# Block 0's gated products: multiplied, transposed and split ahead of the first fast pair, with the pair's first weights loaded early

## The chip, the core and the metric

The kernel runs on one core of one Trainium2 chip. The metric is the device time of one execution in microseconds, the median over several runs. The engines named here are PE (matrix products), DVE and POOL (elementwise work), ACT (casts and activations) and SP, which only issues transfers in this kernel. Each engine works through its own instructions in the order in which they are written, and waits for another engine or a transfer through semaphores.

## What is computed

One trunk layer on x of 256 tokens by 2048 channels, in float32 (the attention and convolution in between are left out):

```python
xn = rms_norm(h, norm1_g)
proj = xn @ w_in                       # q, k, v and the convolution's two gates
...
h = h + concat([att, u]) @ w_out
hn = rms_norm(h, norm2_g)
a  = hn @ w_gate                       # 2048 x 5632
bu = hn @ w_up                         # 2048 x 5632
h  = h + (silu(a) * bu) @ w_down       # 5632 x 2048
```

The change lies in the last four lines, at the seam between the first block of columns of the FFN and the others.

## The kernel before

**Products of split numbers.** Every float32 operand of a product is split into a high part (rounded to the multiplier's format fp32r) and a low part (the rest). A product is three matmuls: high by high, high by low, low by high. For weights, ACT casts the high part (`whi`, L334), and DVE subtracts to get the low part (`wlo`, L343). Part of the low halves are made by ACT and an accumulating transfer on POOL's queue instead (L337, L338). Activations have their halves in `lhi` and `llo`, or, for the normed state `hn`, in the forms that `make_forms` makes.

**Blocks.** The 5632 columns are 11 blocks of N = 512. Block 0 is plain: first all of `w_gate`, then all of `w_up`, 16 row tiles each, in chunks of two row tiles (one raw load of 0.5 MB, one cast, one subtract, 12 matmuls). Blocks 1 to 10 are fast blocks: part of their rows are multiplied in pairs by a scheme of seven products in place of eight. A pair needs one load of 1 MB (`load_pair`, tile `wb`), sums of its parts on DVE (`pair_sums`, `wt`, L1004 to L1006), a cast on ACT (`round_pair`, `wh`, L1010 and L1011) and a subtract on DVE (`split_pair`, `wl`, L1015 and L1016), and is then 21 matmuls (`multiply_pair`, L1032 to L1034). The remaining rows go in units of 12 matmuls (L1050, L1051, L1055). `FIRST = "gugusgsUsGsU"` gives the order of a half of block 1: g and u are units of the gate and of the up columns, s is a pair, and a capital letter is a unit whose low weights come by the transfer. So four units come ahead of block 1's first pair. The blocks form groups of 4, 4 and 3; behind each group stand its products with `w_down`.

**Order of work.** The tile framework keeps the order of the code for each engine. `run_chunks` sets that order: while it multiplies chunk t it runs loads, pair sums, casts and subtracts ahead by fixed numbers of chunks (`LOAD_AHEAD, DMA_AHEAD, SUMS_AHEAD, HI_AHEAD, LO_AHEAD = 9, 5, 5, 4, 3`), from `AHEAD` chunks before the first fast chunk on. Raw loads have four buffers. Everything else that must run beside the chunks is a generator which `resume()` moves on by a step, twice in every chunk or unit; `lag(n)` is n such steps.

**The seam.** Behind the residual's last columns, DVE, POOL and ACT make the second norm's factor (`rstd2`; L218 on POOL is its last step). Then `make_forms` works on `hn` step by step while PE multiplies the up half of block 0: it scales `hn`, and makes `chi`, `clo` for the units and `fhi`, `flo` for the pairs. `hn` lies in the two buffers of the pool `early` that `load_pair` uses for `wb` later. When the up half's sums are complete, `up_done` multiplies `a = ps * rstd2 * silu` on DVE (L872). `transposed` then transposes `a` on PE in two groups of four (L905, outputs `ps_a`), copies the high half on ACT and subtracts the low half on DVE (`llo`, L912). PE's accumulator banks for these transposes come from the same pool `acc_ps` as block 0's sums. The pair's products go into banks that these use as well, so it depends on `llo`.

For the fast blocks, `block_done` ends with the sum of the two halves and the gate (`sum`, L1152), waits some steps, and calls `transposed` as well: five steps, but three in the last block of each group (blocks 3, 7 and 10), with banks of the pool `aux_ps`.

Of the kernel before, what the change touches and what calls it, by code (L numbers as in the profile page):

```python
# [13 lines left out]
F32 = mybir.dt.float32  # L14
# [94 lines left out]
def tile_block(  # L109
# [345 lines left out]
    def run_chunks():  # L455
        n = len(chunks)
        pair_at.extend(i for i, c in enumerate(chunks) if "sides" in c)
        two_at.extend(i for i, c in enumerate(chunks) if "kind" in c and "sides" not in c)
        at = dict(part=0, dma=0, sums=0, round=0)
        first = next(i for i, c in enumerate(chunks) if "kind" in c)  # L460

        def until(what, do, stop, only=lambda c: True, may=lambda i: True):
            while at[what] < min(n, stop) and may(at[what]):
                if only(chunks[at[what]]):
                    do(at[what])
                at[what] += 1

        for t in range(n):
            if t >= first - AHEAD:
                until("part", part_of, t + 1 + LO_AHEAD)  # L470
                until("sums", sums_of, t + 1 + SUMS_AHEAD, may=may_sum)
                until("dma", round_of, t + 1 + DMA_AHEAD, lambda c: c["by_dma"])
                until("round", round_of, t + 1 + HI_AHEAD)
                load_until(t + 1 + LOAD_AHEAD)
            else:
                until("part", part_of, t + 1 + (1 if t < len(XPARTS) else AHEAD))
            part_of(t)
            chunks[t]["multiply"](chunks[t])
            if chunks[t].get("prompt") and chunks[t]["done"]:
                resume()  # L480
        while running:
            resume()
# [382 lines left out]

    def up_done(j, ps):
        fp = ffn["pool"]
        yield
        aa = []
        for m in range(NM):  # L870
            a = fp.tile([P, N], F32, tag=f"sum{2 + m}", name="a")
            dve.scalar_tensor_tensor(a, ps[m], rstd2[m], sil[m], ALU.mult, ALU.mult)  # L872
            aa.append(a)
        yield
        yield from transposed(j, aa)

    def group_of(j):
        return next((g for g in range(len(FGROUPS)) if j < sum(FGROUPS[: g + 1])), None)
# [15 lines left out]
    def transposed(j, aa):  # L894
        g = group_of(j)
        if g not in down:
            place(g)
        d = down[g]
        for t in range(N // P // 2):
            pool_, tag = (aux_ps, "aux") if j else (acc_ps, "acc")  # L900
            pt = pool_.tile([P, 2, S], F32, tag=tag, name="ps_a")
            for i in range(2):
                for m in range(NM):
                    c = (2 * t + i) * P
                    pe.transpose(pt[:, i, m * P : (m + 1) * P], aa[m][:, c : c + P], ident)  # L905
            if (j, t) in d["pairs"]:
                yield from pair_forms(j, t, pt)
            else:
                hi, lo = d["at"][j, t]
                act.copy(hi, pt)  # L910
                yield from lag(3 if j else 2)
                dve.tensor_tensor(lo, pt, hi.bitcast(F32), ALU.subtract)  # L912
            d["ready"].add((j, t))
            yield from lag(2 if j else 1)

    def pair_forms(j, t, pt):

        fp = ffn["pool"]
        q = down[group_of(j)]["pairs"].index((j, t))
        fhi, flo = (f[:, :, q] for f in down[group_of(j)]["forms"])  # L920
        a = fp.tile([P, 2, NM, P], F32, tag="sum0", name="af")
        act.copy(a, pt)
        a11, a21, a12, a22 = a[:, 0, 0], a[:, 0, 1], a[:, 1, 0], a[:, 1, 1]
        act.copy(fhi[:, :2], a[:, :, 0])
        act.activation(fhi[:, 2], a22, AF.Copy, scale=-1.0)
        yield from lag(2)
        f = fp.tile([P, 4, P], F32, tag="sum2" if j else "sum1", name="fs")
        dve.scalar_tensor_tensor(f[:, 1], a21, -1.0, a22, ALU.mult, ALU.subtract)
        dve.scalar_tensor_tensor(f[:, 2], f[:, 1], -1.0, a11, ALU.mult, ALU.subtract)
        dve.tensor_tensor(f[:, 3], a11, a21, ALU.subtract)  # L930
        dve.tensor_tensor(f[:, 0], a12, f[:, 2], ALU.subtract)
        act.copy(fhi[:, 3:], f)
        yield from lag(2)
        dve.tensor_tensor(flo[:, :2], a[:, :, 0], fhi[:, :2].bitcast(F32), ALU.subtract)
        dve.scalar_tensor_tensor(flo[:, 2], a22, -1.0, fhi[:, 2].bitcast(F32), ALU.mult, ALU.subtract)
        yield
        dve.tensor_tensor(flo[:, 3:], f, fhi[:, 3:].bitcast(F32), ALU.subtract)
# [2 lines left out]

    def make_forms():
        fp = ffn["pool"]
        rep = fp.tile([P, S], F32, tag="sum1", name="rep")
        for m in range(NM):
            act.activation(rep[:, m * P : (m + 1) * P], ident, AF.Identity, bias=rstd2[m], scale=0.0)
        yield
        ps = aux_ps.tile([P, N], F32, tag="aux", name="ps_r")
        for m in range(NM):
            pe.transpose(ps[:, m * P : (m + 1) * P], rep[:, m * P : (m + 1) * P], ident)
        yield  # L950
        rb = fp.tile([P, S], F32, tag="sum2", name="rb")
        act.copy(rb, ps[:, :S])
        yield
        for i in range(2):
            for k in range(0, HK, 4):
                t = hn[i][:, k : k + 4, :]
                dve.tensor_tensor(t, t, rb.unsqueeze(1).to_broadcast([P, 4, S]), ALU.mult)
                yield

        nr = HK - NS  # L960
        chi = fp.tile([P, 2 * nr, S], F32R, tag="chi", name="chi")
        clo = fp.tile([P, 2 * nr, S], F32R, tag="clo", name="clo")
        for i in range(2):
            act.copy(chi[:, i * nr : (i + 1) * nr], hn[i][:, NS:])
        yield
        for i in range(2):
            dve.tensor_tensor(clo[:, i * nr : (i + 1) * nr], hn[i][:, NS:],
                              chi[:, i * nr : (i + 1) * nr].bitcast(F32), ALU.subtract)
            yield
        forms.update(plain={k: (chi[:, i, :], clo[:, i, :]) for i, k in enumerate(REST)})  # L970
        a11, a21 = (hn[0][:, :NS, m * P : (m + 1) * P] for m in range(NM))
        a12, a22 = (hn[1][:, :NS, m * P : (m + 1) * P] for m in range(NM))
        fhi = fp.tile([P, 7, NS, P], F32R, tag="fhi", name="fhi")
        flo = fp.tile([P, 7, NS, P], F32R, tag="flo", name="flo")
        f = fp.tile([P, 7, NS, P], F32, tag="wh", name="sums", bufs=2)[:, :4]
        dve.scalar_tensor_tensor(f[:, 1], a21, -1.0, a22, ALU.mult, ALU.subtract)
        dve.scalar_tensor_tensor(f[:, 2], f[:, 1], -1.0, a11, ALU.mult, ALU.subtract)
        act.copy(fhi[:, 0], a11)
        act.copy(fhi[:, 1], a12)
        act.activation(fhi[:, 2], a22, AF.Copy, scale=-1.0)  # L980
        yield
        dve.tensor_tensor(f[:, 3], a11, a21, ALU.subtract)
        dve.tensor_tensor(f[:, 0], a12, f[:, 2], ALU.subtract)
        act.copy(fhi[:, 3:], f)
        yield
        for i, a in ((0, a11), (1, a12)):
            dve.tensor_tensor(flo[:, i], a, fhi[:, i].bitcast(F32), ALU.subtract)
        yield
        dve.scalar_tensor_tensor(flo[:, 2], a22, -1.0, fhi[:, 2].bitcast(F32), ALU.mult, ALU.subtract)
        yield  # L990
        dve.tensor_tensor(flo[:, 3:], f, fhi[:, 3:].bitcast(F32), ALU.subtract)
        forms.update(hi=fhi, lo=flo)

    def load_pair(c):
        c["b"] = early.tile([P, 4, N], F32, tag="wb", name="wb")
        src = weights([(w, k, col, N) for w, col in c["sides"] for k in c["ks"]])
        sp.dma_start(out=c["b"].rearrange("p k n -> p (k n)"), in_=src)

# [146 lines left out]
    def block_done(j, q):  # L1145
# [4 lines left out]
            dve.tensor_tensor(u[m], q[i], u[m], ALU.add)  # L1150
        for m in range(NM):
            dve.tensor_tensor(u[m], u[m], g[m], ALU.mult)  # L1152
        yield from lag(TO_TRANSPOSE if group_of(j) == group_of(j + 1) else 3)
        yield from transposed(j, u)

    def add_to_out(m, n, t):
# [58 lines left out]
    for g, nb in enumerate(FGROUPS):  # L1215
        for j in range(j0, j0 + nb):
            if j:
                gate_up_block(j, FIRST if j == 1 else ORDER)
                continue

            block("w_gate", j * N, range(KD), fh, silu_done)
            block("w_up", j * N, range(KD), fh, lambda ps, j=j: up_done(j, ps))
        for n in range(0, D // N, 2):
            down_block(g, n)
        j0 += nb
# [40 lines left out]
```

## Time and profile before

| | us |
|---|---|
| median of 3 runs | 1077.01 (1076.92 to 1077.07) |
| profiled execution | 1075.79 |
| its span | 1074.0 |
| PE busy | 1044.6 (97%) |
| DVE busy | 900.4 (84%) |
| ACT busy | 654.0 (61%) |
| POOL busy | 129.9 (12%) |
| mean granted clock of PE | 0.993 of full speed |

The span is the time from the first to the last instruction that the profiler recorded; the profiled execution's own time is 1.8 us more. The granted clock is the share of PE's full clock that the chip let it have; in the stretches of this trace that lie wholly in one state it is 1.00 or 0.50. In the rows of the timeline the brackets give the idle time of the engine ahead of the instruction, and what ended it. Names behind an arrow are the program's tiles.

### The profile page before, as it was taken

What the parts mean: (1) busy time and instruction counts of PE and PEld (TensorE: products, weight loads), DVE (VectorE), ACT (ScalarE), POOL (GpSimd) and SP (SyncE); (2) the same over time, 40 slices, a digit from 0 to 9 for tenths busy, and PEclk for the clock granted to TensorE, in tenths of its full rate; (3) what the DMA queues carried; (4) which work ended last, traced back from release to release, by engine and by line L of the source; (5) the groups of instructions that cost most, each with busy time, mean ns of one, the idle gap of its engine ahead of it and who ended that gap; (6) DMA issues with size and microseconds to landing.
All of it is one profiled execution on the core that took longest, in us unless ns stands there. A gap on an engine that the chain in (4) does not pass through costs nothing.

```text
span 1074.0 us, 13249 instructions
## 1 busy us (share of the span) xinstructions
PE 1044.6 (97%) x4780; PEld 861.5 (80%) x4780; DVE 900.4 (84%) x1124; ACT 654.0 (61%) x831; POOL 129.9 (12%) x176
## 2 busy tenths in 40 slices
PE   7999999999999996999999999999999999999898
PEld 7888888877888875787878888888878888888786
DVE  4799989898766677989887788899986897989994
ACT  6644566755756555575765465765755756658551
POOL 0020112200100100010101120100101121001011
PEclk9999999999999998999999999999999999999999
DMA  8656554454457566887959998979878999889774
GB/s 300 211 182 200 184 189 161 154 167 158 146 182 239 167 227 184 273 231 227 310 161 320 264 296 289 287 208 327 235 234 247 260 309 334 240 238 270 238 201 93
DMA packets 62445, 245.47 MB, mean 229 GB/s; under 512 B 6964, under 2 KB 8430, under 8 KB 54956
## 3 DMA queue, kind: packets, MB, share of 16 engines
q1 hardware_dynamic: 48576, 200.56, 52.8%
q0 software_dynamic: 13744, 44.05, 21.5%
q8 instruction: 37, 0.61, 0.2%
q14 instruction: 28, 0.23, 0.1%
q10 hardware_dynamic: 60, 0.03, 0.0%
HBM read 236.22 MB, written 8.39 MB: 228 GB/s over the span
## 4 chain that ended last, share of the span: by engine, by line
PE 55%; DVE 7%; issue 2%; ACT 1%; DMA 1%; DVEq 0%; SPq 0%; ACTq 0%
PE q L1050 10%; PE q L1051 10%; PE q L1055 10%; PE q L1032 8%; PE q L1033 8%; PE q L1034 8%; DVE wl L1016 1%; DVE wlo L343 1%; PE ps_a L905 1%; DVE wt L1004 1%; DMA wb<-in_wts_dram 1%; DVE wt L1005 0%; ACT whi L334 0%; DVE wl L1015 0%; ACT wh L1011 0%
## 5 line engine op out<-in xcount | busy, mean ns | idle before, releaser
L334 ACT CAST whi<-raw 128x1024 fp32r<-128x1024 f32 (+1 forms) x261 | 269.1, 1047 | 122.1 <-PE q L1051 59.2
L343 DVE TENSOR_TENSOR wlo<-raw,whi 128x1024 fp32r<-128x1024 f32 (+1 forms) x193 | 233.7, 1218 | 73.3 <-ACT whi L334 70.5
L373 PE MATMUL acc<-whi,lhi 128*128 128x512 f32 (+1 forms) x448 | 167.6, 379 | 3.6 <-ACT lhi L240 2.9
L374 PE MATMUL acc<-whi,llo 128*128 128x512 f32 (+1 forms) x448 | 165.7, 375 | 0.5 <-DVE llo L241 0.4
L1015 DVE TENSOR_TENSOR wl<-wb,wh 128x1536 fp32r<-128x1536 f32 x58 | 101.7, 1753 | 42.5 <-ACT wh L1010 42.5
L1016 DVE TENSOR_TENSOR wl<-wt,wh 128x2048 fp32r<-128x2048 f32 x58 | 132.7, 2287 | 1.0
L1011 ACT CAST wh<-wt 128x2048 fp32r<-128x2048 f32 x58 | 110.8, 1910 | 35.3 <-DVE wt L1006 35.0
L1050 PE MATMUL q<-whi,chi 128*128 128x512 f32 x320 | 125.7, 393 | 0.0
L1051 PE MATMUL q<-whi,clo 128*128 128x512 f32 x320 | 124.9, 390 | 0.0
L338 POOL DMA_DIRECT2D wlo<-in_wts_dram x68 | 60.9, 895 | 527.6 <-ACT wlo L337 423.1
L1032 PE MATMUL q<-wh,fhi 128*128 128x512 f32 x280 | 110.8, 396 | 6.8 <-DVE llo L912 4.5
L379 PE MATMUL acc<-wlo,lhi 128*128 128x512 f32 (+1 forms) x448 | 114.4, 380 | 1.8 <-DVE wlo L343 1.8
L1033 PE MATMUL q<-wh,flo 128*128 128x512 f32 x280 | 110.0, 393 | 0.0
L1034 PE MATMUL q<-wl,fhi 128*128 128x512 f32 x280 | 109.9, 392 | 0.0
L569 DVE SCALAR_TENSOR_TENSOR y<-upad,cw,y 128x256 f32<-128x256 f32 x240 | 103.8, 483 | 3.4 <-ACT y L562 2.9
L1010 ACT CAST wh<-wb 128x1536 fp32r<-128x1536 f32 x58 | 85.4, 1473 | 32.0 <-issue 23.5
L373 PEld LDWEIGHTS acc<-whi,lhi 128*128 128x128 f32 x448 | 84.3, 188 | 19.3 <-ACT lhi L240 3.3
L374 PEld LDWEIGHTS acc<-whi,llo 128*128 128x128 f32 x448 | 84.4, 188 | 15.7 <-DVE llo L241 0.9
L379 PEld LDWEIGHTS acc<-wlo,lhi 128*128 128x128 f32 x448 | 79.6, 188 | 17.3 <-DVE wlo L343 3.1
L1055 PE MATMUL q<-wlo,chi 128*128 128x512 f32 x320 | 87.3, 395 | 0.0
L1004 DVE TENSOR_TENSOR wt<-wb 128x1024 f32<-128x1024 f32 x58 | 70.8, 1221 | 4.2 <-DMA wb<-in_wts_dram 3.6
L337 ACT ACTIVATE wlo<-raw 128x1024 fp32r<-128x1024 f32 x68 | 71.8, 1056 | 0.2 <-PE q L1055 0.2
(213 smaller groups left out, 1694.9 us busy)
## 6 DMA issues: line engine op xcount, KB each, us to landing
raw<-in_wts_dram SPq DMA_DIRECT2D x259, 512.0 KB, 5.3
wb<-in_wts_dram SPq DMA_DIRECT2D x58, 1024.0 KB, 7.5
wlo<-in_wts_dram POOLq DMA_DIRECT2D x68, 512.0 KB, 8.9
out_dram<-sum POOLq DMA_DIRECT2D x22, 256.0 KB, 7.4
out_dram<-h POOLq DMA_DIRECT2D x8, 256.0 KB, 5.7
h<-in_x_dram SPq DMA_DIRECT2D x6, 256.0 KB, 7.3
h<-in_x_dram SPq DMA_DIRECT2D x4, 128.0 KB, 3.4
raw<-in_wts_dram SPq DMA_DIRECT2D x2, 256.0 KB, 4.1
```

What stands on the lines that cost most here:

```text
L334: act.copy(c["hi"], c["raw"])
L343: dve.tensor_tensor(c["lo"], c["raw"], c["hi"].bitcast(F32), ALU.subtract)
L373: pe.matmul(ps[m], xhi[:, ms], hi[:, j, :], start=c["first"] and j == 0, stop=False)
L374: pe.matmul(ps[m], xlo[:, ms], hi[:, j, :], start=False, stop=False)
L379: pe.matmul(ps[m], xhi[:, ms], lo[:, j, :], start=False, stop=c["last"] and j == nk - 1)
L1016: dve.tensor_tensor(c["lo"][:, :4], c["t"], c["hi"][:, :4].bitcast(F32), ALU.subtract)
L1032: pe.matmul(ps, fhi[:, f, p, :], c["hi"][:, w], start=bool(first), stop=False)
L1033: pe.matmul(ps, flo[:, f, p, :], c["hi"][:, w], start=False, stop=False)
L1034: pe.matmul(ps, fhi[:, f, p, :], c["lo"][:, w], start=False, stop=bool(last))
L1050: pe.matmul(ps, plain[i][0][:, ms], hi[:, i, :], start=i == 0 and bool(c["first"].get(qs[m])), stop=False)
L1051: pe.matmul(ps, plain[i][1][:, ms], hi[:, i, :], start=False, stop=False)
L1055: pe.matmul(sum_bank(c, qs[m]), plain[i][0][:, ms], lo[:, i, :], start=False, stop=i == 1 and bool(c["last"].get(qs[m])))
```

## The change

In the diff, line numbers are left out; the lines move by up to 18 in the file after it.

```diff
@@ run_chunks
-                until("sums", sums_of, t + 1 + SUMS_AHEAD, may=may_sum)
+                until("sums", sums_of, t + 1 + (SUMS_AHEAD if t >= first else 0), may=may_sum)
                 until("dma", round_of, t + 1 + DMA_AHEAD, lambda c: c["by_dma"])
-                until("round", round_of, t + 1 + HI_AHEAD)
+                until("round", round_of, t + 1 + (HI_AHEAD if t >= first else LO_AHEAD))
@@ up_done
-        yield
         aa = []
         for m in range(NM):
             a = fp.tile([P, N], F32, tag=f"sum{2 + m}", name="a")
             dve.scalar_tensor_tensor(a, ps[m], rstd2[m], sil[m], ALU.mult, ALU.mult)
             aa.append(a)
-        yield
-        yield from transposed(j, aa)
+        yield from lag(2)
+        place(0)
+        pts = []
+        for t in range(NB // 2):
+            pts.append(acc_ps.tile([P, 2, S], F32, tag="acc", name="ps_a"))
+            transpose_two(pts[t], aa, t)
+        for t in range(NB // 2):
+            act.copy(down[0]["at"][j, t][0], pts[t])
+        yield
+        for t in range(NB // 2):
+            hi, lo = down[0]["at"][j, t]
+            dve.tensor_tensor(lo, pts[t], hi.bitcast(F32), ALU.subtract)
+            down[0]["ready"].add((j, t))
@@ transposed   (now for fast blocks only: banks of aux_ps, lag(3) and lag(2))
...
@@ make_forms
         fp = ffn["pool"]
+        load_pair(chunks[pair_at[0]])
...
                 dve.tensor_tensor(t, t, rb.unsqueeze(1).to_broadcast([P, 4, S]), ALU.mult)
-                yield
+                yield from lag(1 if i == 0 else 2)
...
                               chi[:, i * nr : (i + 1) * nr].bitcast(F32), ALU.subtract)
-            yield
+            yield from lag(2)
...
         act.activation(fhi[:, 2], a22, AF.Copy, scale=-1.0)
-        yield
+        yield from lag(2)
...
         act.copy(fhi[:, 3:], f)
-        yield
+        yield from lag(2)
@@ load_pair
-        c["b"] = early.tile([P, 4, N], F32, tag="wb", name="wb")
+        if "b" in c:
+            return
+        if c is chunks[pair_at[0]]:
+            c["b"] = ffn["pool"].tile([P, 7, N], F32, tag="wl", name="wb0", bufs=2)[:, :4]
+        else:
+            c["b"] = early.tile([P, 4, N], F32, tag="wb", name="wb")
@@ block_done
-        yield from lag(TO_TRANSPOSE if group_of(j) == group_of(j + 1) else 3)
+        yield from lag(TO_TRANSPOSE)
@@ the calls for block 0
             block("w_up", j * N, range(KD), fh, lambda ps, j=j: up_done(j, ps))
+            chunks[-1]["prompt"] = True
```

In words: the weights of block 1's first pair are loaded at the start of `make_forms`, into one of the two `wl` buffers of the FFN's pool rather than behind `hn`'s release. `make_forms` takes six steps more. Until the first fast chunk, casts run three chunks ahead rather than four, and no pair sums are made ahead. `up_done` multiplies `a` at once when the up half's last chunk is done, transposes all eight pieces in one place two steps later, and makes both low halves a step behind. The last block of each group waits five steps ahead of its transposes, like the others. (`pair_forms` also takes its scratch tile under one tag always.)

On SP's queue, at the start of `make_forms`, the order of the loads before was this (the numbers count the program's tiles; `raw_3620` is a chunk of the up half):

```order
L330 DMA raw_3563<-in_wts_dram 128x1024
L330 DMA raw_3591<-in_wts_dram 128x1024
L330 DMA raw_3620<-in_wts_dram 128x1024
L330 DMA raw_3643<-in_wts_dram 128x1024
L330 DMA raw_3663<-in_wts_dram 128x1024
L330 DMA raw_3683<-in_wts_dram 128x1024
```

In the changed kernel:

```order
L330 DMA raw_3563<-in_wts_dram 128x1024
L330 DMA raw_3591<-in_wts_dram 128x1024
L1015 DMA wb0_3617<-in_wts_dram 128x2048
L330 DMA raw_3622<-in_wts_dram 128x1024
L330 DMA raw_3645<-in_wts_dram 128x1024
L330 DMA raw_3665<-in_wts_dram 128x1024
L330 DMA raw_3684<-in_wts_dram 128x1024
```

The first pair's load now stands ahead of four raw loads of the up half. It waits for all users of the memory that the FFN's pool takes over, POOL's last step of `rstd2` among them. Before, it stood 14 raw loads further back.

On DVE, from the forms' last subtract to the first pair's low halves, the order before was this:

```order
L991 TENSOR_TENSOR flo<-sums,fhi 128x2048
L343 TENSOR_TENSOR wlo<-raw,whi 128x1024 x6
L1004 TENSOR_TENSOR wt<-wb 128x1024
L1005 TENSOR_TENSOR wt<-wb,wt 128x512
L1006 TENSOR_TENSOR wt<-wt,wb 128x512
L343 TENSOR_TENSOR wlo<-raw,whi 128x1024
L872 SCALAR_TENSOR_TENSOR a<-acc,rstd_0_83,sil 128x512
L872 SCALAR_TENSOR_TENSOR a<-acc,rstd_1_84,sil 128x512
L1015 TENSOR_TENSOR wl<-wb,wh 128x1536
L1016 TENSOR_TENSOR wl<-wt,wh 128x2048
```

Behind these rows stood the second pair's sums, a `wlo`, the first `llo` (L912), a further `wl` and sums, and the second `llo`. In the changed kernel:

```order
L1004 TENSOR_TENSOR flo<-sums,fhi 128x2048
L343 TENSOR_TENSOR wlo<-raw,whi 128x1024 x3
L871 SCALAR_TENSOR_TENSOR a<-acc,rstd_0_83,sil 128x512
L871 SCALAR_TENSOR_TENSOR a<-acc,rstd_1_84,sil 128x512
L343 TENSOR_TENSOR wlo<-raw,whi 128x1024
L1022 TENSOR_TENSOR wt<-wb_3617 128x1024
L1023 TENSOR_TENSOR wt<-wb_3617,wt 128x512
L1024 TENSOR_TENSOR wt<-wt,wb_3617 128x512
L1033 TENSOR_TENSOR wl<-wb_3617,wh 128x1536
L1034 TENSOR_TENSOR wl<-wt,wh 128x2048
L1022 TENSOR_TENSOR wt<-wb 128x1024
```

Two further rows of the second pair's sums follow, and then both `llo` together (L884). The products `a` have moved ahead of the first pair's sums, and both `llo` ahead of the second pair's `wl`. On PE all eight transposes now stand behind block 1's first unit; before, four stood in the second unit and four behind the third.

On PE at the end of block 3, where the products with `w_down` start, four matmuls (L905) transposed the first half of the gated sums behind the second of a pair's seven products before:

```order
L1033 MATMUL q_4933<-wh,llo 128x512
L1034 MATMUL q_4933<-wl,lhi 128x512
L905 MATMUL ps_a<-ident,sum_4858 128x128
L905 MATMUL ps_a<-ident,sum_4860 128x128
L905 MATMUL ps_a<-ident,sum_4858 128x128
L905 MATMUL ps_a<-ident,sum_4860 128x128
L1032 MATMUL q_4943<-wh,lhi 128x512
```

In the changed kernel:

```order
L1051 MATMUL q_4913<-wh,llo 128x512
L1052 MATMUL q_4913<-wl,lhi 128x512
L891 MATMUL ps_a<-ident,sum_4858 128x128
L891 MATMUL ps_a<-ident,sum_4860 128x128
L891 MATMUL ps_a<-ident,sum_4858 128x128
L891 MATMUL ps_a<-ident,sum_4860 128x128
L1050 MATMUL q_4957<-wh,lhi 128x512
```

They stand behind the sixth product, 12 matmuls later, and the second four move back by as much. Block 7 moves in the same way, block 10 by somewhat more.

More of the change, by code (lines that the diff above doesn't have):

```diff
@@ L873, in up_done, with transpose_two @@
             aa.append(a)
-        yield
-        yield from transposed(j, aa)
+        yield from lag(2)
[6 more added lines that the diff above has]
+            act.copy(down[0]["at"][j, t][0], pts[t])
+        yield
+        for t in range(NB // 2):
+            hi, lo = down[0]["at"][j, t]
+            dve.tensor_tensor(lo, pts[t], hi.bitcast(F32), ALU.subtract)
+            down[0]["ready"].add((j, t))
+    def transpose_two(pt, aa, t):
+        for i in range(2):
+            for m in range(NM):
+                c = (2 * t + i) * P
+                pe.transpose(pt[:, i, m * P : (m + 1) * P], aa[m][:, c : c + P], ident)
     def group_of(j):
@@ L899, in transposed @@
         for t in range(N // P // 2):
[L900 to L905, printed above, removed]
+            pt = aux_ps.tile([P, 2, S], F32, tag="aux", name="ps_a")
+            transpose_two(pt, aa, t)
             if (j, t) in d["pairs"]:
@@ L910, in transposed @@
                 act.copy(hi, pt)
-                yield from lag(3 if j else 2)
+                yield from lag(3)
                 dve.tensor_tensor(lo, pt, hi.bitcast(F32), ALU.subtract)
             d["ready"].add((j, t))
-            yield from lag(2 if j else 1)
+            yield from lag(2)
     def pair_forms(j, t, pt):
@@ L926, in pair_forms @@
         yield from lag(2)
-        f = fp.tile([P, 4, P], F32, tag="sum2" if j else "sum1", name="fs")
+        f = fp.tile([P, 4, P], F32, tag="sum2", name="fs")
         dve.scalar_tensor_tensor(f[:, 1], a21, -1.0, a22, ALU.mult, ALU.subtract)
@@ L984, in make_forms @@
         act.copy(fhi[:, 3:], f)
-        yield
+        yield from lag(2)
         for i, a in ((0, a11), (1, a12)):
```

## Prediction

> **What bounds the kernel now.** I began with the page's first part: PE is busy for 97% of the span, so time can come only out of the 3% in which it stands, or out of stretches in which it is busy at a low clock.
>
> ```profile
> span 1074.0 us, 13249 instructions
> PE 1044.6 (97%) x4780; PEld 861.5 (80%) x4780; DVE 900.4 (84%) x1124; ACT 654.0 (61%) x831; POOL 129.9 (12%) x176
> ```
>
> Next came the view by stretches (start and end in us, length, busy time of PE, PEld, DVE, ACT and POOL, then the granted clock, the DMA share and GB/s). The first two rows are the up half of block 0 and the stretch from its end to the end of block 1's first pair; the other three are places where the clock was halved.
>
> ```profile
> 364.00:397.00 33.00, 32.30 (x141) 25.80 (x140) 26.75 (x26) 19.86 (x24) 0.38 (x1) 1.00 0.57 182
> 397.00:427.50 30.50, 21.36 (x79) 16.66 (x79) 22.14 (x21) 14.31 (x14) 1.82 (x2) 0.83 0.75 238
> 406.90:410.20 3.30, 3.30 (x10) 2.71 (x10) 3.30 (x2) 2.60 (x4) 0.00 (x0) 0.50 0.26 42
> 422.30:427.30 5.00, 5.00 (x12) 3.94 (x13) 0.00 (x0) 0.00 (x0) 0.00 (x0) 0.50 0.63 142
> 1011.10:1014.40 3.30, 3.30 (x10) 2.53 (x8) 3.23 (x6) 3.30 (x3) 0.00 (x0) 0.50 0.02 5
> ```
>
> In the up half PE works almost without a pause at full clock. In the 30.5 us behind it, PE stands 9.1 us, and two stretches run at half clock. The timeline of PE gives the pace and the stands (start, length, count, and in brackets the idle time ahead with what ended it).
>
> ```profile
> 368.99 0.39 PE L373 MATMUL acc<-whi,lhi 128*128 128x512 f32 x1
> 371.71 0.39 PE L373 MATMUL acc<-whi,lhi 128*128 128x512 f32 x1
> 396.13 1.07 PE L379 MATMUL acc<-wlo,lhi 128*128 128x512 f32 x4
> 406.10 0.33 PE L905 MATMUL ps_a<-ident,a 128*128 128x128 f32 x1 [4.36 <-DVE a L872]
> 422.25 0.79 PE L1032 MATMUL q<-wh,fhi 128*128 128x512 f32 x1 [4.45 <-DVE llo L912]
> 427.45 0.39 PE L1050 MATMUL q<-whi,chi 128*128 128x512 f32 x1
> ```
>
> The two rows of L373 begin neighbouring chunks of 12 matmuls: 371.71 - 368.99 = 2.72 us, 0.227 us a matmul. The up half's last four start at 396.13 and end at 397.0. From there to 427.45 are 30.4 us, for work that at this pace needs 4 units (10.9) + the transposes (about 1) + 21 matmuls (4.8) = 16.7 us. PE waits first for DVE's products `a`, then for the low half `llo` of their transposes. So DVE bounds this place, and its row of work from 366 to 422 is what the change has to shorten. The chain there, with the waits inside it up to the first `a`:
>
> ```profile
> 366.08 2.45 DVE L343 TENSOR_TENSOR wlo<-raw,whi 128x1024 fp32r<-128x1024 f32 x2 [3.32 <-ACT whi L334]
> 401.57 1.23 DVE L1004 TENSOR_TENSOR wt<-wb 128x1024 f32<-128x1024 f32 x1 [2.73 <-DMA wb<-in_wts_dram]
> 403.55 0.69 DVE L1006 TENSOR_TENSOR wt<-wt,wb 128x512 f32<-128x512 f32 x1
> 405.30 1.40 DVE L872 SCALAR_TENSOR_TENSOR a<-acc,rstd,sil 128x512 f32<-128x512 f32 x2
> 406.62 1.75 DVE L1015 TENSOR_TENSOR wl<-wb,wh 128x1536 fp32r<-128x1536 f32 x1
> 408.28 2.28 DVE L1016 TENSOR_TENSOR wl<-wt,wh 128x2048 fp32r<-128x2048 f32 x1
> 421.52 0.68 DVE L912 TENSOR_TENSOR llo<-ps_a,lhi 128x512 fp32r<-128x512 f32 x1
> DVE wlo L343 <- ACT whi L334: 5.0, 2, 3.3
> DVE wt L1004 <- DMA wb<-in_wts_dram: 2.7, 1, 2.7
> DVE wlo L343 <- PE acc L374: 2.4, 1, 2.4
> ```
>
> **The change, part by part. (1) The early load.** It stands on SP's queue ahead of four raw loads and waits there for the buffers' last users, the latest of which is POOL's second `rstd`. What it is moved past, and how long transfers take:
>
> ```profile
> 357.81 0.33 SPq L330 DMA_DIRECT2D raw<-in_wts_dram  x1
> 362.78 0.33 SPq L330 DMA_DIRECT2D raw<-in_wts_dram  x1
> 363.82 0.56 POOL L218 TENSOR_TENSOR rstd<-rsq,neghalf 128x1 f32<-128x1 f32 x1
> 365.01 1.03 ACT L334 CAST whi<-raw 128x1024 fp32r<-128x1024 f32 x1
> DMA to landing us min/median/max: 3.3/3.3/3.3
> DMA to landing us min/median/max: 5.0/5.0/5.0
> DMA to landing us min/median/max: 8.5/8.5/8.5
> DMA to landing us min/median/max: 10.6/10.6/10.6
> ```
>
> The four landings are a raw load (0.5 MB) into idle queues at 367.4, a first-pair-sized load (1 MB, `wb`) into idle queues at 430.7, a raw load behind a `wb` at 394.3, and a `wb` behind both at 394.7. Before, the raw loads of this place went out between 357.81 and 362.78 (one earlier still). Now none goes before 364.38, when `rstd` ends. The 1 MB takes 5.0, and the raw load behind it another 1.7 to 2.5 (estimates: 5.0 - 3.3 for the half MB more, and what the queued `wb`, issued 0.4 after the raw load, took beyond it for a whole MB, 10.6 + 0.4 - 8.5). So it lands near 364.5 + 5.0 + 1.7 = 371.2, and its cast (1.03), with what it waits for its semaphore, ends near 372.4. PE wanted those weights at 368.99: it stands 3.4 us, and I add half a halved window, since the windows above are 3.3 long and lose half of that. Had the early load the queued one's 10.6 and the raw load 2.5 behind it, the cast would end at 378.6; if the raw load overlapped it completely (364.5 + 3.3 + 1.0), at 369.
>
> **(2) DVE up to the products.** Before: 366.08 to 405.30, 39.2 us, with idle time of 5.0 - 3.3 (that part lies ahead of 366.08) + 2.7 + 2.4 = 6.8. The new order has three things fewer ahead of `a`: the idle 6.8, the pair's sums (1.23 + 2 x 0.69 = 2.6) and one `wlo` (1.2): 28.6 us of work are left. It gains waits: the new chunks' casts come only just ahead of their subtracts (0.45 and one cast of 1.05, since the casts are now made three chunks ahead, not four), and the widened steps put a cast in ACT's row behind that of the form sums. That cast's row:
>
> ```profile
> 382.45 1.91 ACT L984 CAST fhi<-sums 128x2048 fp32r<-128x2048 f32 x1 [2.56 <-DVE sums L983]
> 404.28 1.90 ACT L1011 CAST wh<-wt 128x2048 fp32r<-128x2048 f32 x1 [1.24 <-DVE wt L1006]
> ```
>
> 1.91 + 1.03 = about 3 us. So 372.4 (its start, moved by part 1) + 28.6 + 4.5 = 405.5. The products thus come no earlier than before: what the order saves, the late load takes.
>
> **(3) DVE from the products to `llo`.** Now behind `a` (405.5 to 407.0): one `wlo` 1.2, the first pair's sums 2.6 (no wait, its weights landed long ago), `wl` 1.75, the wait for ACT's second cast (1.9 from the sums' end, which covers `wl`) and 2.28, the second pair's sums 2.6, then both `llo` 2 x 0.65: 407.0 + 1.1 + 2.6 + 1.9 + 2.3 + 2.6 + 1.3 = 418.8, where before it was 422.2: 3.4 us earlier. Of the 12 matmuls that wait for it, 5.2 us before (427.45 - 422.25, at half clock), 2.7 are left if PE comes to the wait without a long stand. PE: the up half ends near 401.5 (397.0 + 3.4 + what is lost of the halved window), a unit to 404.2, a stand of about 2.5 for `a`, transposes (1), three units (8.2) and the pair's first 9 matmuls (2.0) bring it to 418.1. It stands 0.7 there, too short to halve anything. First pair's end: 418.8 + 2.7 = 421.6 against 427.45, **-5.9**. If the stand for `a` halves a window, PE comes at 419.8 and the term shrinks by 1.0; I take 0.4 of it, **+0.4**. The rows for whether it halves:
>
> ```profile
> 1009.56 0.33 PE L905 MATMUL ps_a<-ident,sum 128*128 128x128 f32 x1 [2.47 <-DVE sum L1152]
> 1010.16 0.33 PE L905 MATMUL ps_a<-ident,sum 128*128 128x128 f32 x1 [0.28 <-DVE sum L1152]
> ```
>
> A stand of 2.47 us was followed by clock 0.50 in the row of 1011.10. The Trainium skill (TensorE: Matmul & The Clock Gate, Part 1: The HAM clock gate) has the clock drop only after at least one idle window of about 3.4 us; by that rule a stand of 2.5 costs nothing more and the sum would be 0.4 lower. Here the trace shows a halved clock after a shorter stand, so the measurement decides.
>
> **(4) What is given back at the end of block 1's first half.** DVE now carries one `wlo` (1.2), one pair's `wl` (1.75 + 2.28) and one pair's sums (2.6), together 7.8 us, behind `llo` that it had ahead of it. Its idle time up to the next place where PE needs it:
>
> ```profile
> DVE wl L1015 <- ACT wh L1010: 8.1, 3, 6.7
> DVE wlo L343 <- ACT whi L334: 0.5, 1, 0.5
> 453.15 0.47 PE L1032 MATMUL q<-wh,fhi 128*128 128x512 f32 x1 [0.38 <-DVE sum L1130]
> ```
>
> 8.6 us of it can take the 7.8, but DVE starts only 3.4 us earlier while PE starts 5.9 earlier. DVE reaches `sum` at 452.3 - 3.4 + 7.8 - 8.6 = 448.1; PE reaches it at 452.35 - 5.9 = 446.5: **+1.6**. Bounds: 0 if more idle time lies behind that row, +5.9 if only half of the 8.6 can be used.
>
> **(5) The last blocks of the groups.** The transposes of blocks 3 and 7 stand 12 matmuls later, those of block 10 later by a unit's 8 and some.
>
> ```profile
> 545.37 0.33 PE L905 MATMUL ps_a<-ident,sum 128*128 128x128 f32 x1 [0.46 <-DVE sum L1152]
> ```
>
> That wait and a second one of 0.28 behind it go in block 3, and the like in block 7: 0.75 to 0.95 each, say -1.7. In block 10 the 2.47, the 0.28 and half of the 3.3 us window (1.65) go, 4.4 in all. What is late next there: the second transposes take the buffer that the first `llo` frees, and this `llo` now stands behind a `wl` on DVE (4 us), so PE gets 2 to 3.5 back. I take -0.9 (0 to -4.4). Together **-2.6**.
>
> The look-ahead, the tag of the form sums and the shared helper cost nothing by themselves: the first is in (2), the others move no instruction.
>
> **Sum.** -5.9 + 0.4 + 1.6 - 2.6 = -6.5. The profiled execution took 1075.79 (span 1074.0), 1.2 below the median of 1077.01; the sum is against its rows, and as a difference it carries over: 1077.0 - 6.5 = **1070.5**.
>
> **Rivals.** *Raw loads in time.* If the early load held the raw loads back little (the 369 above), DVE starts at 366.1, the last `llo` comes at 412.5 and the pair ends at 415.2: -12.2, with +1.6 and -2.6, 1063.8. For it: the transfers' share of the engines is 0.57 in the up half, there is room. Against: SP's queue waits in order, and 1 MB ahead cost the raw load at 394.3 its 8.5 in place of 3.3.
>
> *No difference.* If the raw loads behind the early one take as long as the queued ones, the cast ends at 378.6 and everything behind is 6.2 later: 1076.7. The same comes from halved windows: each is 1.65, and three new stands (for the cast, for `a`, at the transposes of block 10) have one each at most, 1075.5.
>
> *Slower.* The first pair's `llo` now stands on DVE behind the second pair's sums, so behind the landing of that pair's weights. Their load stands on SP behind the last raw loads of the up half and goes out near 403 (an estimate: those buffers come free with the last `wlo` ahead of `a`); the sums want it at 414.9. Landing in 5.0 to 10.6 it is there at 408 to 414. Each us past 414.9 costs one: at 421.4 the gain is gone, and from 423.5 the kernel is slower, 1079.2 and up. For it: 10.6 leaves under 1 us of room, and the transfers' share is 0.75 there. Against: deciding needs a landing 20 us after the issue, twice the longest shown.
>
> **How the numbers follow.** Forecast 0.66, raw loads in time 0.10, no difference 0.15, slower 0.09. The forecast's own range, by the bounds of (2) to (5), is 1066.5 to 1074.5. The range takes in the first rival's middle and most of the third: 1063.5 to 1077.5; outside stay about half of the 0.10, the 0.09 and a little of the 0.15. A measurement tells about 0.2% (2.15 us) from no change, so faster is below 1074.9 and slower above 1079.2: 0.76, 0.15 and 0.09.
>
> **What the changed profile would show.** Right: a stand of PE near 369, of 3 to 4 us, released by a cast `whi`; the first `a` between 404 and 407; a last `llo` near 419 with PE standing under 1 us for it; no halved clock at the end of the first pair, which ends near 421.6; waits for `sum` at the next first half of 1.5 to 2.5 us; no 2.47 ahead of block 10's transposes but 2 to 3 us ahead of the second ones. Wrong: no stand at 369 (then 1064), a cast `whi` past 378, or DVE waiting long for a `wb` between `wl` and `llo`.

## The result and the profile after

The changed kernel took 1069.88 us (median; 1069.52 to 1071.39), the kernel before 1077.04: a ratio of 0.9937, 95% interval 0.9917 to 0.9956. The forecast was 1070.5. One of the four executions of the kernel before was slow, at 1161.32 us, and the ratio leaves it out. The changed kernel's profiled execution took 1070.12 with a span of 1068.3; the one of before 1075.79 with 1074.0. So the two traces differ by 5.7 us, where the medians differ by 7.2; what follows adds up to the 5.7, to rounding.

The view by stretches shows first where the time came from (columns as above; the first two rows answer to the first two there, the third and the last are new halved windows, the fourth is DVE's stretch from the last `llo` to the next `sum`):

```profile
364.00:397.00 33.00, 30.19 (x125) 24.07 (x124) 21.15 (x22) 19.03 (x23) 0.60 (x2) 0.95 0.65 225
397.00:427.50 30.50, 28.20 (x126) 22.65 (x126) 29.59 (x27) 18.02 (x16) 1.82 (x2) 1.00 0.70 228
372.00:375.40 3.40, 3.40 (x9) 2.67 (x10) 3.40 (x3) 2.87 (x4) 0.00 (x0) 0.54 0.91 316
417.50:449.50 32.00, 28.36 (x125) 23.08 (x123) 29.15 (x24) 19.43 (x16) 2.59 (x3) 1.00 0.94 283
449.70:453.10 3.40, 3.40 (x10) 2.50 (x11) 3.33 (x6) 1.33 (x2) 0.00 (x0) 0.66 0.84 242
```

In the seam (397 to 427.5) PE is busy for 28.2 us at full clock, where it was busy for 21.4 at 0.83. In the up half it lost some: it stands 2.8 us there, 0.7 before, and a window is halved. PE's stands, each with what ended it, from the timeline:

```profile
371.97 0.53 PE L373 MATMUL acc<-whi,lhi 128*128 128x512 f32 x1 [2.50 <-ACT whi L334]
405.00 0.33 PE L891 MATMUL ps_a<-ident,a 128*128 128x128 f32 x1 [1.21 <-DVE a L871]
416.97 0.50 PE L1050 MATMUL q<-wh,fhi 128*128 128x512 f32 x1 [0.76 <-DVE llo L884]
449.66 0.47 PE L1050 MATMUL q<-wh,fhi 128*128 128x512 f32 x1 [3.80 <-DVE sum L1148]
1013.63 0.33 PE L891 MATMUL ps_a<-ident,sum 128*128 128x128 f32 x1 [1.03 <-DVE llo L924]
1017.95 0.50 PE L1069 MATMUL q<-whi,llo 128*128 128x512 f32 x1 [0.68 <-DVE llo L924]
```

The stands of 4.36 and 4.45 in the seam are 1.21 and 0.76 now. The first row is the price of the early load, the fourth is what DVE gives back. Following the same matmul in both traces (start after less start before) gives this account; PE does the same 4780 matmuls in both:

| up to | shift, us | of it here |
|---|---|---|
| the up half, 361 | +0.3 | +0.3 (an offset of this execution from its first matmuls on) |
| the up half, behind the stand at 372 | +4.7 | +4.4 |
| the end of the first pair | -6.9 | -11.6 |
| block 1's second half | -2.5 | +4.4 |
| block 2's second half | -3.5 | -1.0 |
| behind block 3 | -4.4 | -0.9 |
| before block 7's end | -3.9 | +0.5 (near 707, in no part that was changed) |
| behind block 7 | -4.8 | -0.9 |
| the end | -5.7 | -1.0 (block 10) |

What set the stand at 372 shows on POOL, SP, ACT and the transfers (the first landing is that of the early load, the second that of the raw load issued at 366.86, the last of the four behind it):

```profile
364.12 0.56 POOL L218 TENSOR_TENSOR rstd<-rsq,neghalf 128x1 f32<-128x1 f32 x1
364.71 0.33 SPq L1015 DMA_DIRECT2D wb<-in_wts_dram  x1
366.86 0.41 SPq L330 DMA_DIRECT2D raw<-in_wts_dram  x1
370.87 1.04 ACT L334 CAST whi<-raw 128x1024 fp32r<-128x1024 f32 x1 [5.46 <-DMA raw<-in_wts_dram]
371.95 1.23 DVE L343 TENSOR_TENSOR wlo<-raw,whi 128x1024 fp32r<-128x1024 f32 x1 [8.88 <-ACT whi L334]
DMA to landing us min/median/max: 4.8/4.8/4.8
DMA to landing us min/median/max: 7.7/7.7/7.7
404.20 0.75 DVE L871 SCALAR_TENSOR_TENSOR a<-acc,rstd,sil 128x512 f32<-128x512 f32 x1
416.23 1.28 DVE L884 TENSOR_TENSOR llo<-ps_a,lhi 128x512 fp32r<-128x512 f32 x2
```

The early load waits for POOL until 364.7 and four raw loads go out only behind it. ACT stands 5.5 us for the first of them, and DVE stands 8.9 for the cast: its long row starts at 371.95 where it started at 366.08. The products still begin at 404.2 (405.3 before), and both `llo` end by 417.5 (422.2 before).

### The profile page after: what moved, and what is told of

Read it like the earlier page. It is cut to its first block, busy times and chain, and to the rows that moved or that the text cites. A ratio compares the mean times of both kernels' runs of the same rounds, so it can differ in the third digit from the quotient of the medians.

```text
span 1068.3 us, 13248 instructions
## 1 busy us (share of the span) xinstructions
PE 1043.2 (98%) x4780; PEld 860.2 (81%) x4780; DVE 899.5 (84%) x1124; ACT 653.4 (61%) x831; POOL 130.7 (12%) x176
## 4 chain that ended last, share of the span: by engine, by line
PE 51%; DVE 10%; issue 2%; ACT 2%; DMA 1%; DVEq 0%; SPq 0%; ACTq 0%
PE q L1069 9%; PE q L1068 9%; PE q L1073 9%; PE q L1050 7%; PE q L1051 7%; PE q L1052 7%; DVE wl L1034 2%; DVE wt L1022 1%; DVE wlo L343 1%; DVE wt L1023 1%; PE acc L373 1%; PE acc L374 1%; DVE wl L1033 1%; PE ps_a L891 1%; PE acc L379 1%
```

## The experiments

My theory was the one of the prediction: DVE's row of work, from the first subtract after the second norm on, sets both the seam and the next place where PE needs DVE. The main rival was that the early load is what pays. Each run was timed beside the kernel before on its chip; the ratio is to that. The profiled executions differ from each other by a fixed time that they have by 20 us and keep up to 366, ahead of all that the change touches: 0.2 to 2.0 us later than the trace before. It is called the offset below. The whole change's is 0.3.

**The early load, later.** In `make_forms`:

```diff
-        load_pair(chunks[pair_at[0]])
         rep = fp.tile([P, S], F32, tag="sum1", name="rep")
...
                 yield from lag(1 if i == 0 else 2)
+        load_pair(chunks[pair_at[0]])
```

> The changed kernel, but the first pair's early load is made nine steps later in make_forms (behind the scaling of hn), so that on SP's queue five more raw loads stand ahead of it. Theory (DVE's row of work from 366 on sets the seam, and the early load as placed delays its start by 6 us): no stand of PE near 372, DVE starts at 366 rather than 372, the first product near 398.5, the first pair ends near 414.5, 5 us earlier than in the changed kernel; the stand at the next first half stays 3 to 4 us, since DVE bounds it too; median near 1064.5. Rival (the delay is hidden behind other waits, as the first product comes no earlier than 404): 1069 to 1070.

It took 1065.3 us, ratio 0.9895 (0.988 to 0.9909). Rows of DVE and PE:

```profile
367.27 1.23 DVE L343 TENSOR_TENSOR wlo<-raw,whi 128x1024 fp32r<-128x1024 f32 x1 [3.31 <-ACT whi L334]
399.52 0.74 DVE L871 SCALAR_TENSOR_TENSOR a<-acc,rstd,sil 128x512 f32<-128x512 f32 x1
412.29 0.50 PE L1050 MATMUL q<-wh,fhi 128*128 128x512 f32 x1 [0.78 <-DVE llo L884]
444.51 0.60 PE L1050 MATMUL q<-wh,fhi 128*128 128x512 f32 x1 [3.33 <-DVE sum L1148]
```

No stand near 372. DVE starts 4.7 us earlier, and the products, `llo` and the next `sum` are 4.7, 4.7 and 5.2 earlier (this execution's offset is 0.9 more than the changed kernel's, so without it each is 0.9 more). A shift that passes almost unchanged through 80 us of DVE's row fits DVE bounding all of it. By itself it does not show that, since PE loses its stand at 372 in the same run; that DVE ends each of PE's later stands points the same way. The place of the load cost 4.6 us in the medians (1069.88 and 1065.3). Whether the load pays at all, the next run tells.

**No early load at all.** `load_pair` at the start of `make_forms` and its branch for the `wl` buffer removed:

```diff
-        load_pair(chunks[pair_at[0]])
...
-        if c is chunks[pair_at[0]]:
-            c["b"] = ffn["pool"].tile([P, 7, N], F32, tag="wl", name="wb0", bufs=2)[:, :4]
-        else:
-            c["b"] = early.tile([P, 4, N], F32, tag="wb", name="wb")
+        c["b"] = early.tile([P, 4, N], F32, tag="wb", name="wb")
```

> The changed kernel without the early load: the first pair's weights come into the pool early behind hn's release, as before; all else as changed. Theory: DVE starts at 366 as in the run with the later load; the first pair's load goes out near 396 and lands 5 to 10 us later, DVE wants it at 401, so 1 to 6 us of the gain of 5 are lost again: 1065 to 1070, not slower than the changed kernel. Rival (the early load is what pays): the sums wait long for the weights, 1073 or more.

1066.06 us, ratio 0.9893 (0.9873 to 0.9914): as fast as with the later load. DVE's waits from 366 to 412 hold no transfer:

```profile
DVE wlo L343 <- ACT whi L334: 7.2, 3, 3.3
DVE wl L1030 <- ACT wh L1025: 0.3, 1, 0.3
```

With the products ahead of the sums, the weights are wanted late enough to come the old way. I had expected 1 to 6 us to be lost by that. The medians differ by 0.8, less than these runs can tell, and at the seam the traces show no loss: offsets taken off, the first pair ends 12.8 us earlier than in the kernel before with the later load and with none. The rival is out.

**The hoist alone, and the load alone, on the kernel before.** The first takes `up_done` and its helper from the changed kernel:

```diff
 def up_done(j, ps):
-        yield
...
-        yield from transposed(j, aa)
+        yield from lag(2)
+        place(0)
+        ... (as in the change)
             block("w_up", j * N, range(KD), fh, lambda ps, j=j: up_done(j, ps))
+            chunks[-1]["prompt"] = True
```

> The kernel before with the new up_done alone: products, eight transposes and both low halves in one place, load, steps, look-ahead and group ends as before. Theory (the order on DVE from the products to llo is the gain): the products near 404.5, the last llo near 415 rather than 422, the first pair ends between 419.6 and 421.3, DVE gives up to 2 us back at the next first half: 1070 to 1073. Rival (the hoist needs the early weights, since the sums stay ahead of the products): 1075 or more.

The second takes only `load_pair`'s call and branch:

```diff
 def make_forms():
         fp = ffn["pool"]
+        load_pair(chunks[pair_at[0]])
```

> The kernel before with the early load alone, at the place where the change puts it. Theory: the cast near 369 comes 5.9 later and DVE starts by as much later, the wait of 2.7 for the weights goes, so the products and all behind them are 3.2 us later: 1079 to 1081. Rival (the wait of 2.7 for the weights is saved): 1074.3.

The hoist alone: 1070.68 us, ratio 0.9945 (0.993 to 0.9959). The load alone: 1079.88, ratio 1.0032 (1.002 to 1.0043), slower. PE's rows, of the hoist first, then of the load:

```profile
405.50 0.47 PE L891 MATMUL ps_a<-ident,a 128*128 128x128 f32 x1 [4.33 <-DVE a L871]
447.83 0.47 PE L1048 MATMUL q<-wh,fhi 128*128 128x512 f32 x1 [0.39 <-DVE sum L1146]
```

```profile
373.49 0.51 PE L373 MATMUL acc<-whi,lhi 128*128 128x512 f32 x1 [2.37 <-ACT whi L334]
392.74 0.80 PE L373 MATMUL acc<-whi,lhi 128*128 128x512 f32 x1 [2.38 <-ACT whi L334]
426.64 0.80 PE L1038 MATMUL q<-wh,fhi 128*128 128x512 f32 x1 [6.04 <-DVE llo L912]
```

With the hoist alone PE still stands 4.33 for the products but not at all for `llo`, and only 0.39 for the next `sum`; that comes at 447.8, while the whole change has it at 449.7. Take one matmul of block 2, at 504.88 in the trace before, and take the offsets off: it comes 6.6 us earlier with the hoist alone, 3.8 earlier with the whole change, and 9.9 and 9.8 earlier in the runs with the later load and with none. So the hoist carries the whole net gain at the seam, and more; by the ratios alone (0.9945, and 0.9964 for the whole change without its gain at the group ends, below) this would be at the edge of the intervals. With the load alone that matmul comes about 1.6 later. The load adds a stand at 373, and makes DVE so late that the casts stall PE again at 393 (ACT has them behind the form sums' cast, which waited 2.55 us for DVE). `llo` comes 4.4 us later, of which 2.0 are this execution's offset.

**The other two parts at the seam.** Steps of `make_forms` as narrow as before, all else as changed:

```diff
-                yield from lag(1 if i == 0 else 2)
+                yield
...
-            yield from lag(2)
+            yield
```

(and at the two places behind the form sums' casts in the same way.)

> The changed kernel with make_forms in steps as narrow as before. Theory (DVE's sum of work up to the products sets them, and it stays the same): the idle time in the chain 4.1 or less instead of 3.9, the products within 1 us of 404.2, 1069 to 1071. Rival (the wide steps are needed to keep the raw chunks' subtracts in time): PE stands in the up half, 1073 or more.

1070.55 us, ratio 0.9948 (0.9933 to 0.9963): no difference from the whole change that these runs can tell. The products begin at 404.26 (404.20), though PE stands 1.06 and 0.33 us more inside the up half, which its shorter stand behind it takes up.

The old look-ahead:

```diff
-                until("sums", sums_of, t + 1 + (SUMS_AHEAD if t >= first else 0), may=may_sum)
+                until("sums", sums_of, t + 1 + SUMS_AHEAD, may=may_sum)
-                until("round", round_of, t + 1 + (HI_AHEAD if t >= first else LO_AHEAD))
+                until("round", round_of, t + 1 + HI_AHEAD)
```

> The changed kernel with the look-ahead of before in run_chunks: the first pair's sums (2.6 us) stand ahead of the products again. Theory (DVE's sum of work sets llo and the next first half's sum): products 2.6 later, PE reaches the pair's second part 1.9 us later than llo, so the first pair ends 1.9 later, but the stand of 3.8 at the next first half shrinks by as much and nothing is lost there: 1068.5 to 1070.5. Rival (what the seam loses is carried to the end): 1071.8 to 1073.5.

1070.89 us, ratio 0.9948 (0.9932 to 0.9965), 0.4 above my theory's range and 0.9 below the rival's. The rows:

```profile
408.75 0.47 PE L891 MATMUL ps_a<-ident,a 128*128 128x128 f32 x1 [3.82 <-DVE a L871]
451.13 0.47 PE L1050 MATMUL q<-wh,fhi 128*128 128x512 f32 x1 [0.38 <-DVE sum L1148]
```

This execution is 1.2 us later than the changed one's by its offset. Beyond that the products come 2.6 later (PE's transposes 408.75 against 405.00), PE's stand for them is 3.82 in place of 1.21, and the first pair ends 3.7 later. But the stand for the next `sum` is 0.38 in place of 3.80, and behind it nothing of the 3.7 is left. A loss at the seam was gone 30 us later: beside the early load, DVE's row sets the end, whichever of the two orders stands ahead of it.

Both results hold beside the early load only. Without it, the hoist alone had its matmul of block 2 6.6 us earlier, and the hoist with these two parts 9.8. With the hoist alone DVE has this wait between 366 and 405:

```profile
DVE wt L1020 <- DMA wb<-in_wts_dram: 2.6, 1, 2.6
```

In the run without the early load it has none for a transfer up to 452. So the new look-ahead, which puts the first pair's sums behind the products, hides the wait that the early load was meant to remove. No run has the look-ahead and the hoist without the wider steps, so its own share of the 3.2 us is not measured.

**The group ends.** Three steps again in the last block of each group:

```diff
-        yield from lag(TO_TRANSPOSE)
+        yield from lag(TO_TRANSPOSE if group_of(j) == group_of(j + 1) else 3)
```

> The changed kernel with three steps rather than five ahead of the transposes in blocks 3, 7 and 10. Theory: the waits for sum of 0.46 + 0.28 come back in blocks 3 and 7, the 2.47 and a halved window in block 10, and the wait for llo there goes: 0.9 + 0.9 + 1.0 slower, near 1072.7. Rival (the five steps only move the wait): 1069.9.

1072.37 us, ratio 0.9964 (0.9953 to 0.9976): 2.5 above the whole change. The two intervals just touch, but the rows agree: the stands of 0.44, 0.47 and 2.50 for `sum` are back at 542, 794 and 1006, and this trace falls behind the changed one's by 0.9, 0.9 and 1.0 at these places.

**One subtract less behind `llo`.** `FIRST` with the unit behind the first pair as a capital:

```diff
-FIRST = "gugusgsUsGsU"
+FIRST = "gugusGsUsGsU"
```

> The changed kernel with the unit behind block 1's first pair made by the transfer: its low weights on ACT and POOL's queue rather than on DVE (FIRST has G in the sixth place). Theory (DVE has work without a gap from llo to the next first half's sum and so sets the stand of 3.8 us there): one subtract of 1.2 us less, the stand near 2.6, and the halved window may go as well: 1067.5 to 1068.8. Rival (ACT's casts and the transfers set it): ACT has 1.05 more, the stand stays or grows, 1070 to 1071.

1068.62 us, ratio 0.9927 (0.9912 to 0.9943), which the intervals do not tell from the whole change; the rows do. PE's stand, and the clock behind it:

```profile
448.55 0.47 PE L1050 MATMUL q<-wh,fhi 128*128 128x512 f32 x1 [1.63 <-DVE sum L1148]
448.50:451.90 3.40, 2.98 (x12) 2.04 (x13) 3.33 (x6) 1.33 (x2) 0.00 (x0) 1.00 0.82 241
```

The stand falls from 3.80 to 1.63, and no window is halved. The subtract is 1.2 of that; most of the rest is a wait of 1.23 us for a cast `wh`, which DVE had at 433.46 and has no longer. About 1 us of this comes back at block 2, whose stand is 1.28 again as before the change. ACT has more work in this run and DVE less, so DVE's row, with its waits for casts in it, sets this stand, and not the amount of ACT's work.

**Together.** The later load and the G:

> The later early load and the G in the sixth place of FIRST together. Theory (both shorten DVE's row ahead of the next first half's sum, the first by 5 and the second by 1.2): the stand there falls from 3.3 to about 1.5 and halves no window: 1062.5 to 1064. Rival (ACT or the transfers take over): 1065 or more.

1063.02 us, ratio 0.9881 (0.9867 to 0.9894): the lowest median of all, though the interval overlaps those of the other runs with a later load or none. Against the change's 0.9937 that is 0.56% or 6 us less. The stand for `sum` is 1.64. With the fourth unit by the transfer as well (`FIRST = "gugUsGsUsGsU"`):

> As the one before, and the fourth unit's low weights by the transfer too (U in the fourth place of FIRST). Theory: DVE loses another 1.2 us, the stand at the next first half falls to 0.4 or less: 1061.5 to 1063. Rival (the transfers ahead of the first pairs are late, their share is 1.0 there): 1064 or more.

1064.6 us, ratio 0.9891 (0.9876 to 0.9906), not better; the theory missed. Two rows of PE and one of DVE:

```profile
402.09 0.33 PE L891 MATMUL ps_a<-ident,a 128*128 128x128 f32 x1 [1.36 <-DVE a L871]
443.40 0.47 PE L1050 MATMUL q<-wh,fhi 128*128 128x512 f32 x1 [1.55 <-DVE sum L1148]
400.15 1.23 DVE L343 TENSOR_TENSOR wlo<-raw,whi 128x1024 fp32r<-128x1024 f32 x1 [1.21 <-ACT whi L334]
```

The subtract saved on DVE was replaced by a wait of 1.21 us for a cast, ahead of which ACT now makes that unit's low weights (1.06). The products come later, not earlier: 401.29 against 399.68 in the run before, of which 0.3 is offset. One subtract less stands behind them, so by block 2 only 0.2 us is lost. Another 1.4 us is lost near 950, far behind the changed unit, and no run says why. The time lies in the rival's range, but the wait shown is for ACT and not for a transfer. Last, the later load and the G with four steps in block 10 (`TO_TRANSPOSE if j < 10 else 4`):

> The later load and the G, and in block 10 four steps rather than five ahead of the transposes. Theory: the waits for llo of 1.0 and 0.7 behind it shrink, the wait for sum ahead of the first transposes comes back by less: 0 to 1 faster than without, 1062 to 1064. Rival (the wait for sum comes back whole with its halved window): 1 slower, 1064 to 1065.

1063.13 us, ratio 0.989 (0.9875 to 0.9906): no difference. The waits for `llo` in block 10 go, and waits of 0.22 and 0.28 for `sum` stand there again, with a window at half clock behind them (0.50 from 998.1 to 1001.4); the end of that trace is 0.3 later than with five steps.

## Why the prediction was right, step by step

The time came out 0.6 us below the forecast, but with two terms off by more than that, of opposite sign. By the traces, whose rows the sum was made from, the change gave 5.7 where 6.5 was forecast: the profiled execution lies 1.2 below the median before and 0.2 above it after. So the closeness of the time is partly luck, and the terms have to be looked at one by one.

*The early load* was right in kind: the raw load landed behind it, the cast ended at 371.9 (forecast 372.4), and the window behind the stand was halved (0.54). The waiting matmul came at 371.97, where 368.99 and this execution's offset of 0.3 was its turn: 2.7 late, not 3.4, as the cast was half a us earlier than forecast and the rest is the offset. The halved window makes it the 4.4 of the table.

*DVE up to the products*: 404.2, forecast 405.5. Of that 0.45 is the earlier start and 0.6 the waits: I had added 4.5 us of them, and the trace has 3.9, with 2.9 for the cast behind that of the form sums (about 3 forecast). The rest is the row's work, 28.4 in place of 28.6.

*From the products to `llo`*: forecast 418.8, measured 417.5, the same 13.3 us behind the products. One thing in it was wrong: PE needs the first `llo` at 416.9, not the last, and 15 matmuls follow it, not 12. The pair ends at 420.5 (416.97 + 15 x 0.227 = 420.4, and the first of the 15 takes 0.1 longer), forecast 421.6. That PE stood 0.76 for `llo`, with 0.7 forecast, is a coincidence: it came to the wait at 416.2 and not at 418.1, and was let go as much earlier. The stand for the products was 1.2, not 2.5, and halved nothing. The term was -6.9 against before, or -7.2 without the offset; forecast -5.9 + 0.4.

*What is given back* was undersized: +1.6 forecast, +4.4 measured at block 1's second half, of which 1.0 came back at block 2, where a stand of 1.28 shrank to 0.30. The step that failed is "8.6 us of it can take the 7.8". DVE's waits from 417.5 to 449.5 after:

```profile
DVE wl L1033 <- ACT wh L1028: 1.2, 1, 1.2
DVE wl L1034 <- ACT wh L1029: 0.6, 2, 0.3
DVE wlo L343 <- ACT whi L334: 0.6, 1, 0.6
```

So 2.4 us of idle time stay, where the prediction had used up all of the 8.6. The longest of these waits, 1.2, is for a cast that ACT makes behind two other steps, for the first of which it waited for a transfer:

```profile
430.05 1.05 ACT L334 CAST whi<-raw 128x1024 fp32r<-128x1024 f32 x1 [2.87 <-DMA raw<-in_wts_dram]
```

My 448.1 for `sum`, less the 1.3 by which `llo` was earlier, plus 2.4, is 449.2; DVE began it at 448.83, and PE went on at 449.66. The stand grew from 0.38 to 3.80, which is 3.4 of the 4.4, and the halved window behind it (0.66 in the row of 449.70) is the rest. The prediction has PE reach `sum` at 452.35 in the trace before; its row gives 453.15 - 0.38 = 452.77. PE goes on 0.83 behind DVE's start, so the two nearly cancel, and the term is off by 0.1 for it. My bound of +5.9 for this term held it.

*The group ends* were -0.9, -0.9 and -1.0: -2.8 or, taken back alone, 2.5 in the medians; forecast -2.6. The new wait for `llo` in block 10 was there, 1.03 and 0.68, shorter than the 2 to 3.5 I gave it, while a wait of 1.3 for `sum` ahead of it took the rest.

*The rivals.* Raw loads in time did not happen, but the run with the later load shows what it would have given: 1065.3, forecast 1063.8 for it. *No difference* rested in part on three new stands that might each halve a window; only that for the cast did, and the other halved window stood at `sum`, which it had not named. The wait for the second pair's weights did not happen: no row of DVE's waits names a transfer there. Their load went out at 402.42 (near 403 forecast) and landed 5.6 us later, and the sums began at 413.63. (For a landing in 10.6 the room was 1.3 us by the prediction's own numbers, 414.9 - 413.6, and not under 1.)

## What to carry to other kernels

When one engine's row of work runs without a gap from one place to the next, moving a result to its front is only lent: look for where the row is next waited for, and count how much of its idle time there is really usable. A prefetch on an in-order queue is charged with everything behind it: make the queue reach it only when what it waits for is over, or leave it where it was. Undo each part alone, and see what it stood beside: here two of the parts at the seam made no difference next to the early load, while the early load cost 4.6 us of the gain, and next to them it was not needed.

## What the runs showed of the hardware

Stands of PE of nearly one length had different prices. The run with the load alone has both:

```profile
373.40:376.80 3.40, 3.31 (x14) 2.73 (x15) 3.33 (x3) 2.88 (x5) 0.00 (x0) 1.00 0.91 348
392.70:396.10 3.40, 3.36 (x8) 2.67 (x9) 3.38 (x3) 2.83 (x3) 0.00 (x0) 0.53 0.31 110
```

The first follows a stand of 2.37 us and is at full clock; the second follows one of 2.38 and is halved. The changed kernel's 2.50 halved, and the one of 2.47 in the kernel before too. In the traces' clock records the halved windows are 3.41 us long, or twice that, on a raster of 3.41 us: each begins a whole number of such windows behind the others of its trace. The stand of 2.37 lies across two windows of this raster, 0.85 us in one and 1.52 in the next; the stand of 2.38 has 2.1 us in one.

PE's idle time in every window of the raster, from 30 us on in all thirteen traces, divides the windows at full clock almost cleanly. In 25 of them PE was idle for 2.0 us or more, and a halved window followed each. In 3899 it was idle for 1.94 or less, and a halved window followed only one of these (1.60 us idle, the window of the last run above; why is not known). So what counts in these traces is the idle time within one window of the raster, not the length of the stand: a stand that straddles two windows can be spared. No run moved a stand on purpose to test this.

The Trainium skill (TensorE: Matmul & The Clock Gate, Part 1: The HAM clock gate) has the window's length and that it runs freely, and this agrees; that a whole idle window is needed does not: about 2 us of the 3.41 were enough here.
